# Two token tiles of x transposed one after the other, and a pair's gate product and output norm recorded in later pieces

## The chip, the cores and the metric

The kernel runs on one core of one Trainium2 chip. The metric is the device time of one execution in microseconds (us), lower is better; times below are medians of the runs made, or are read from one profiled execution. Engines are named as the profile names them: PE is TensorE's matrix multiply, PEld its weight load, DVE VectorE, ACT ScalarE, POOL GpSimd and SP SyncE, which here only issues DMAs (SPq is its queue).

## What is computed

Two transformer blocks on one sequence of 256 tokens with 1024 features, all float32. The change lies in the first half of the first block, the mixers. Cut to what matters:

```python
def first_block(x, ...):                                # x [1, 256, 1024]
    xn = rms_norm(x, norm1_gain)
    proj = xn @ w_in                                    # 4*512 retention columns, 1792 rwkv columns
    q, k = rotary(proj[..., 0:512]), rotary(proj[..., 512:1024])
    ret = silu(g_ret) * head_norm(retention(q, k, v), ret_gn_gain)
    rw = rwkv7_time_mix(proj[..., 2048:], ...)
    h = x + concat([ret, rw], -1) @ w_out
    h = h + hier_moe(rms_norm(h, norm2_gain), ...)      # 32 experts, top 2
    return rms_norm(h, final_norm_gain)

def rwkv7_time_mix(feats, ...):                         # 8 heads of 64
    f = feats + (previous_token(feats) - feats) * mu
    r, k, v, w_lo, a_lo, g_lo = split(f)
    decay = exp(-exp(-softplus(-(w0 + tanh(w_lo) @ w_up)) - 0.5))
    a, g = sigmoid(a0 + a_lo @ a_up), sigmoid(g_lo) @ g_up
    y = the recurrence over the tokens (state [64, 64] for each head)
    y = head_norm(y, gn_gain, eps)
    bonus = sum(r * k * r_k, -1) * v
    return (y + bonus) * g
```

The second block (two kinds of attention and a product-key feed-forward) follows on the first one's output.

## The kernel before

The program is one straight run of stages: `phase_a` (the mixers and `w_out`, to about 228 us of the profile), `phase_b` (routing and 32 experts, to about 690 us), then the second block.

Every float32 product that needs full precision is done as three faster matmuls of a high and a low part (`mm3`): ACT copies the high part (line 211 for weights, 349 for x), DVE subtracts to get the low part (218 for weights, 351 for x). Weights come as 128x1024 units over SP's queue (line 204), through a generator `ahead`: each `next(ws)` records the high part of one unit, the low part of the one before it, and the load that takes its buffer.

At the start `setup` issues on SP's queue: the first tile of x (128 tokens), the constants `cst` (the identity for PE's transposes is in it), the gains `vec`, the second tile of x; `phase_a` then the first weight units. `row_rstd` squares each tile of x on ACT (343) for the norm's scale, which later goes in as a row `R` (439). `transposed` transposes x in four banks; each bank holds two 128-feature blocks of all 256 tokens, so its four transposes read both tiles of x; `scaled` then takes a bank out in two 128x256 pieces on ACT (349) and two on DVE (351).

After that the order of the instructions is made by hand-written generators, turned by `interleave`: each generator yields how long (by a running sum of estimated PE time) it wants to stand back, or a condition. Those with the earlier place in the list go first. `features` yields the projection, feature tile after feature tile (24 matmuls of 256 columns each: `xt,u` in the trace; DVE then makes `fe`, `d`, `ft`, lines 525 to 529) and four groups of 512 columns (`u,xt`). `rwkv(p, ...)` for p from 0 to 3 is one pair of heads. It makes its decays from `tl,lora` (`sg`, `cs`, lines 596 to 618), its gate `gg` from `gs,gup` (line 604), takes its k, r and v features (624 to 653), solves a triangular system in five levels (`X`, `Z`, `XT`: 701 to 716), carries a state over four chunks (`G`, `Sb`: 733 to 745), and ends with the head norm of its output: s1 and y on DVE (755 to 757), y² on POOL (759), its sum on DVE (760), the reciprocal root on POOL (336, 338), y·r on DVE (762), then after a yield of 5.5 a transposition back on PE (`cst,y`) and gate, bonus, high and low part (768 to 772). Engines run their instructions in the recorded order, so a DVE instruction that waits holds up all that stand behind it.

`out_weights` loads `w_out` (line 393) when pair 3's front is done, `first_experts` begins the loads of expert weights `wB` (line 890) when pair 2's outputs are recorded. All of these loads are on SP's one queue.

Of the kernel before, what the change touches and what calls it, by code (L numbers as in the profile page):

```python
# [15 lines left out]
AF = mybir.ActivationFunctionType  # L16
# [5 lines left out]
S, D = 256, 1024  # L22
# [60 lines left out]
CST_KEPT = 256  # L83

FM_ORDER = [(12, 13), (4, 0), (8, 5), (9, 1), (2, 10), (11, 6), (7, 3)]
WARM = (8, 0, 4, 0, 0, 5, 14, 2)
# [76 lines left out]
class K:  # L163
# [80 lines left out]
    def mm(self, out, l, r, start=True, stop=True, **k):  # L244
        n = 1
        for x in r.shape[1:]:
            n *= x
        m = 1
        for x in l.shape[1:]:
            m *= x  # L250
        self.pe += (max(n, 64) / 2.4e3 * (1 if l.dtype != F32 else 4) + 0.01) * (1 if m > 64 else 0.5)
        self.nc.tensor.matmul(out, l, r, start=start, stop=stop, **k)  # L252
# [55 lines left out]
    def setup(self):  # L308
        nc, i = self.nc, self.i
# [8 lines left out]
        nc.sync.dma_start(self.h[:, 0], i["x"][:, 0])  # L318
        nc.sync.dma_start(self.cst, i["cst"][:, 0:CST_KEPT])
        nc.sync.dma_start(self.vec, i["vec"])  # L320
        nc.sync.dma_start(self.h[:, 1], i["x"][:, 1])
# [47 lines left out]
    def phase_a(self):  # L369
        nc, tc, i = self.nc, self.tc, self.i  # L370
        with ExitStack() as cx:
# [37 lines left out]
            rt = {"qT": T("late", [128, 2, 4, S], "qT"), "v": T("mid", [128, 2, 512], "vr"), "g": T("late", [128, 2, 512], "gr")}  # L409
            rt["rs"] = [self.row_rstd(self.ap["tiny"], self.h[:, t], rt["v" if t else "g"].rearrange("p t d -> p (t d)"), "rows") for t in range(2)]  # L410
            self.transposed([self.h[:, t] for t in range(2)], "norm1_gain", *xt, ws, WARM[1])
# [151 lines left out]
    def rwkv(self, p, zs, lora, gup):  # L563
# [37 lines left out]
        b = self.bank([128, S])  # L601
        mm(b, gup[:, ps], gs, start=True, stop=True)
        gg = L([128, S], "gg", bufs=NBUF)
        nc.scalar.activation(gg, b, AF.Copy)
# [16 lines left out]
        yield lambda: 4 + p in self.got and p in self.got  # L621
        kp, rp = self.got.pop(4 + p), self.got.pop(p)
# [136 lines left out]
        nc.gpsimd.tensor_tensor(y2, y, y, OP.mult)  # L759
        nc.vector.tensor_reduce(s2, y2, AX.X, OP.add)  # L760
        r = self.rstd(self.ap["end"], s2, 64, 4, RWKV_EPS)
        nc.vector.tensor_tensor(y, y, r[:, :, None].to_broadcast([128, 4, 64]), OP.mult)
        yield 5.5
# [7 lines left out]
        nc.scalar.activation(hi, o, AF.Copy)  # L771
        nc.vector.tensor_tensor(lo, o, hi.bitcast(F32), OP.subtract)
# [1097 lines left out]
```

## Time and profile before

| what | before |
|---|---|
| median of 3 runs | 1635.88 us (1634.16 to 1636.99) |
| the profiled execution | 1633.89 us, of which its span is 1632.1 us |
| PE busy over the span | 1581.5 us (97%), 11118 matmul records |
| DVE busy | 967.6 us (59%) |
| ACT busy | 654.9 us (40%) |
| POOL busy | 218.8 us (13%) |
| read from HBM | 386.62 MB, 238 GB/s over the span |

The span is what the trace covers; 1.8 us of the profiled execution lie around it. A share over the span mixes stages with different limits, so the rows further down are taken by stretch. A row of the timeline gives the start, the time until its last instruction ended, the line and what was written and read, with the number of instructions merged; in square brackets stands how long the engine sat idle before it and what released it.

### The profile page before, as it was taken

Reading aid. Unit: us, or ns where it says so; the run is one execution under the profiler, and the core shown is the slowest. Engines: PE = TensorE matmul, PEld = TensorE weight load, DVE = VectorE, ACT = ScalarE, POOL = GpSimd, SP = SyncE. Lnnn points to the kernel's source line nnn. Section 1 sums busy time; section 2 is a strip of 40 time slices with the busy share of each in tenths; the row PEclk is TensorE's granted clock in tenths of the full one; section 3 lists DMA queues with packets and bytes.
Section 4 is the critical chain, followed back from the end, with each engine's and each line's share of the span. In section 5 each row is a group of like instructions: output and inputs, shape, how many; then the busy total and the mean of one; then the engine's idle time right before and its main releaser. Section 6 shows DMA issues by size and latency. Waiting matters only on the chain.

```text
span 1632.1 us, 28041 instructions
## 1 busy us (share of the span) xinstructions
PE 1581.5 (97%) x11118; PEld 1217.2 (75%) x11118; DVE 967.6 (59%) x1845; ACT 654.9 (40%) x1171; POOL 218.8 (13%) x249
## 2 busy tenths in 40 slices
PE   8999999999999999899999999999999999999998
PEld 7888873443444334378799999999999888888887
DVE  6676561121212112289889997788999755555554
ACT  5333341211111111266655556555544444444443
POOL 3213020000000000174210000123444000000000
PEclk9999999999999999999999999999999999999999
DMA  6324699999999999853355556555555566666664
GB/s 204 105 66 142 228 353 391 405 414 420 419 419 419 420 419 420 345 181 117 98 197 167 188 178 194 162 164 168 162 164 166 169 193 193 193 193 193 194 193 156
DMA packets 84297, 390.61 MB, mean 239 GB/s; under 512 B 9632, under 2 KB 9776, under 8 KB 63424
## 3 DMA queue, kind: packets, MB, share of 16 engines
q1 hardware_dynamic: 83088, 384.45, 65.6%
q0 software_dynamic: 928, 3.25, 0.5%
q8 instruction: 90, 1.47, 0.4%
q10 hardware_dynamic: 144, 1.05, 0.2%
q14 instruction: 47, 0.39, 0.1%
HBM read 386.62 MB, written 2.10 MB: 238 GB/s over the span
## 4 chain that ended last, share of the span: by engine, by line
PE 53%; DVE 2%; POOL 2%; issue 1%; ACT 0%; ACTq 0%; DVEq 0%; POOLq 0%
PE b L252 53%; POOL rs_r L338 1%; DVE u L218 1%; PE b L264 1%; DVE g L1727 0%; POOL rs_m L336 0%; POOL y L1418 0%; POOL rs_r L1407 0%; DVE oh L1835 0%; ACT s L1451 0%; DVE h L469 0%; DVE u L1684 0%; DVE ss L1405 0%; DVE qz L1430 0%; DVE mx L1447 0%
## 5 line engine op out<-in xcount | busy, mean ns | idle before, releaser
L211 ACT ACTIVATE u<-u 128x1024 fp32r<-128x1024 f32 x334 | 354.1, 1061 | 388.2 <-PE b L252 366.2
L218 DVE TENSOR_TENSOR u<-u,u 128x1024 fp32r<-128x1024 f32 x334 | 412.5, 1236 | 150.1 <-PE b L252 114.5
L252 PE MATMUL b<-mix,u 128*128 128x256 f32 x3456 | 425.6, 281 | 0.0
L252 PEld LDWEIGHTS b<-mix,u 128*128 128x128 f32 x3456 | 411.1, 188 | 0.0
L252 PE MATMUL b<-u,oh 128*128 128x512 f32 x1536 | 350.3, 390 | 2.0 <-ACT oh L1667 2.0
L252 PEld LDWEIGHTS b<-u,oh 128*128 128x128 f32 x1536 | 289.3, 188 | 62.8 <-ACT oh L1667 2.2
L252 PE MATMUL b<-mr,u 128*64 128x512 f32 x944 | 232.3, 595 | 16.2 <-DMA mr<-in_wB 16.0
L252 PEld LDWEIGHTS b<-mr,u 128*64 128x64 f32 x944 | 74.5, 137 | 158.0 <-issue 120.7
L1130 DVE TENSOR_TENSOR hh<-hh,b 128x512 f32<-128x512 f32 x16 | 11.0, 688 | 230.2 <-PE b L252 230.2
L1711 POOL TENSOR_TENSOR g<-g,gelu 128x4 f32<-128x4 f32 (+43 forms) x87 | 94.2, 1083 | 355.2 <-ACT gelu L1710 348.2
L252 PE MATMUL b<-u,xt 128*128 128x512 f32 x480 | 123.4, 407 | 0.8 <-DVE u L218 0.8
L252 PE MATMUL b<-mr,hT 128*64 128x512 f32 x480 | 115.5, 596 | 3.6 <-DVEq L1194 1.8
L252 PEld LDWEIGHTS b<-u,xt 128*128 128x128 f32 x480 | 89.1, 191 | 21.5 <-DVE u L218 1.1
L1175 DVE SCALAR_TENSOR_TENSOR u<-b,sw,u 128x512 fp32r<-128x512 f32 x32 | 23.9, 750 | 127.8 <-ACT u L1174 127.8
L252 PEld LDWEIGHTS b<-mr,hT 128*64 128x64 f32 x480 | 35.6, 137 | 70.9 <-issue 63.3
L1155 ACT ACTIVATE hT<-b 128x512 f32<-128x512 f32 x16 | 9.6, 598 | 160.1 <-PE b L264 160.1
L1668 DVE TENSOR_TENSOR oh<-g,oh 128x512 fp32r<-128x512 f32 x64 | 44.3, 693 | 41.1 <-ACT oh L1667 41.0
L1174 ACT ACTIVATE u<-b,sw 128x512 fp32r<-128x512 f32 x32 | 21.9, 687 | 105.1 <-PE b L252 105.1
L1303 POOL MEMSET qz<- 128x2048 f32 x2 | 3.5, 1800 | 448.8 <-DVEq L1194 448.8
L1727 DVE TENSOR_TENSOR g<-g,b 128x252 f32<-128x252 f32 (+47 forms) x111 | 61.5, 592 | 0.0
L1835 DVE TENSOR_TENSOR oh<-oh,gw 128x512 f16<-128x512 f16 x128 | 54.6, 465 | 0.0
L1129 ACT ACTIVATE hh<-b 128x512 f32<-128x512 f32 x16 | 9.6, 597 | 99.3 <-PE b L252 99.3
(381 smaller groups left out, 1713.7 us busy)
## 6 DMA issues: line engine op xcount, KB each, us to landing
mr<-in_wB SPq DMA_DIRECT2D x160, 1024.0 KB, 15.2
u<-in_down SPq DMA_DIRECT2D x128, 512.0 KB, 3.7
u<-in_up SPq DMA_DIRECT2D x128, 512.0 KB, 4.3
mr<-in_wB SPq DMA_DIRECT2D x36, 512.0 KB, 15.0
u<-in_wA SPq DMA_DIRECT2D x30, 512.0 KB, 3.7
u<-in_wB SPq DMA_DIRECT2D x28, 512.0 KB, 14.4
u<-in_wC SPq DMA_DIRECT2D x24, 512.0 KB, 4.0
u<-in_wQ SPq DMA_DIRECT2D x16, 512.0 KB, 3.6
```

What stands on the lines that cost most here:

```text
L211: nc.scalar.activation(hi, r, AF.Copy)
L218: nc.vector.tensor_tensor(lo, r, hi.bitcast(F32), OP.subtract)
L252: self.nc.tensor.matmul(out, l, r, start=start, stop=stop, **k)
L264: self.nc.tensor.transpose(out, x, self.ident)
L338: nc.gpsimd.tensor_tensor(r, m, self.mhalf[:, :width], OP.pow)
L1130: nc.vector.tensor_tensor(self.hh, self.hh, bs[1], OP.mult)
L1174: nc.scalar.activation(yh[:, o], b, AF.Copy, scale=sw)
L1175: nc.vector.scalar_tensor_tensor(yl[:, o], b, sw, yh[:, o].bitcast(F32), op0=OP.mult, op1=OP.subtract)
L1668: nc.vector.tensor_tensor(lo, src, hi.bitcast(F32), OP.subtract)
L1711: nc.gpsimd.tensor_tensor(dst[:, 0:n], dst[:, 0:n], g[:, 0:n], OP.mult)
L1727: nc.vector.tensor_tensor(d, d, s, OP.mult)
L1835: self.nc.vector.tensor_tensor(w[:, :, part].rearrange("p t (k x) -> p t k x", x=2), o[:, :, 0].rearrange("p t (k x) -> p t k x", x=2), se ...
```

## The change

Three places. At the start, SP's queue carries the two tiles of x first, and `cst` and `vec` go on ACT's queue. x is transposed tile by tile: a bank now holds four 128-feature blocks of one tile's 128 tokens, so the first two banks need the first tile alone; each bank is taken out in four 128x128 pieces on each of ACT and DVE (16 on each in place of 8). The squares of x (343) and with them the row scales are recorded behind these. In `rwkv`, the gate product `gs,gup` and its copy move from the pair's decays to the place where its k and r features are there. In the output norm, the one yield of 5.5 becomes 1.0, 2.0 and 1.5 around the sum and y·r, and one of 0.75 stands ahead of the low part.

```diff
-        nc.sync.dma_start(self.h[:, 0], i["x"][:, 0])
-        nc.sync.dma_start(self.cst, i["cst"][:, 0:CST_KEPT])
-        nc.sync.dma_start(self.vec, i["vec"])
-        nc.sync.dma_start(self.h[:, 1], i["x"][:, 1])
+        nc.scalar.dma_start(self.cst, i["cst"][:, 0:CST_KEPT])
+        for t in range(2):
+            nc.sync.dma_start(self.h[:, t], i["x"][:, t])
+        nc.scalar.dma_start(self.vec, i["vec"])
...
+            next(ws)
+            for t in range(2):
+                for k4 in range(2):
+                    b = self.bank([128, 4, 128])
+                    for j in range(4):
+                        k = 4 * k4 + j
+                        self.tr(b[:, j], self.h[:, t, k * 128:k * 128 + 128])
+                    ks, o = range(4 * k4, 4 * k4 + 4), slice(t * 128, t * 128 + 128)
+                    self.scaled(b, [(xt[0][:, k, o], xt[1][:, k, o], self.v("norm1_gain", k)) for k in ks])
+                    if t:
+                        next(ws)
             rt["rs"] = [self.row_rstd(...) for t in range(2)]
-            self.transposed([self.h[:, t] for t in range(2)], "norm1_gain", *xt, ws, WARM[1])
+            next(ws)
+            self.warm(WARM[1])
...
-        b = self.bank([128, S])
-        mm(b, gup[:, ps], gs, start=True, stop=True)
-        gg = L([128, S], "gg", bufs=NBUF)
-        nc.scalar.activation(gg, b, AF.Copy)
...
         yield lambda: 4 + p in self.got and p in self.got
+        b = self.bank([128, S])
+        mm(b, gup[:, ps], gs, start=True, stop=True)
+        gg = L([128, S], "gg", bufs=NBUF)
+        nc.scalar.activation(gg, b, AF.Copy)
...
         nc.gpsimd.tensor_tensor(y2, y, y, OP.mult)
+        yield 1.0
         nc.vector.tensor_reduce(s2, y2, AX.X, OP.add)
         r = self.rstd(self.ap["end"], s2, 64, 4, RWKV_EPS)
+        yield 2.0
         nc.vector.tensor_tensor(y, y, r[:, :, None].to_broadcast([128, 4, 64]), OP.mult)
-        yield 5.5
+        yield 1.5
...
         nc.scalar.activation(hi, o, AF.Copy)
+        yield 0.75
         nc.vector.tensor_tensor(lo, o, hi.bitcast(F32), OP.subtract)
```

Since `interleave` counts estimated PE time, the yields move instructions of other generators too. Three places show how.

On DVE at the end of pair 0's outputs (`y`, `s`, `rs_r` are the norm's, `r` the rotary of a retention tile, `fe` to `ft` a feature tile, `u` a weight's low part, `Z` a level of pair 1's solve), the order before:

```order
L757 TENSOR_TENSOR y_1314<-b_1291,s_1315 128x256
L760 TENSOR_REDUCE s_1316<-y_1320 128x4
L762 TENSOR_TENSOR y_1314<-y_1314,rs_r_1325 128x256
L793 TENSOR_TENSOR r_1241<-b_723,rot_131 128x4x64
L794 TENSOR_TENSOR r_1241<-b_723,rot_131 128x4x64
L525 TENSOR_TENSOR fe_46_223<-b_1254,R_260 128x256
L527 TENSOR_TENSOR d_1358<-fe_46_223 128x256
L529 SCALAR_TENSOR_TENSOR ft_1360<-d_1358,vec_83,fe_46_223 128x256
L218 TENSOR_TENSOR u_1364<-u_995,u_1248 128x1024
L707 TENSOR_TENSOR Z_979<-b_1378,cst_80 128x256
```

and the order now, in the same place on DVE:

```order
L770 TENSOR_TENSOR y_1330<-b_1307,s_1331 128x256
L809 TENSOR_TENSOR r_1257<-b_739,rot_131 128x4x64
L810 TENSOR_TENSOR r_1257<-b_739,rot_131 128x4x64
L774 TENSOR_REDUCE s_1332<-y_1336 128x4
L538 TENSOR_TENSOR fe_46_239<-b_1270,R_276 128x256
L540 TENSOR_TENSOR d_1373<-fe_46_239 128x256
L542 SCALAR_TENSOR_TENSOR ft_1375<-d_1373,vec_83,fe_46_239 128x256
L218 TENSOR_TENSOR u_1379<-u_1011,u_1264 128x1024
L720 TENSOR_TENSOR Z_995<-b_1393,cst_80 128x256
L777 TENSOR_TENSOR y_1330<-y_1330,rs_r_1370 128x256
```

The sum of y² now stands behind the two rotary products, and y·r behind the solve's Z; all else keeps its order.

On ACT at the start (`xt` is the transposed x, `gr` and `vr` are scratch for the squares, `u` a weight's high part), the order before:

```order
L343 ACTIVATE gr_137,ss_138<-h_76 128x1024
L343 ACTIVATE vr_136,ss_144<-h_76 128x1024
L349 ACTIVATE xt_13_133<-b_158,vec_83 128x256 x2
L211 ACTIVATE u_167<-u_150 128x1024
L349 ACTIVATE xt_13_133<-b_169,vec_83 128x256 x2
L211 ACTIVATE u_182<-u_152 128x1024
L349 ACTIVATE xt_13_133<-b_184,vec_83 128x256 x2
L349 ACTIVATE xt_13_133<-b_193,vec_83 128x256 x2
```

and now:

```order
L349 ACTIVATE xt_13_133<-b_146,vec_83 128x128 x4
L349 ACTIVATE xt_13_133<-b_159,vec_83 128x128 x4
L349 ACTIVATE xt_13_133<-b_172,vec_83 128x128 x4
L211 ACTIVATE u_185<-u_138 128x1024
L349 ACTIVATE xt_13_133<-b_187,vec_83 128x128 x4
L211 ACTIVATE u_204<-u_140 128x1024
L343 ACTIVATE gr_137,ss_206<-h_76 128x1024
L343 ACTIVATE vr_136,ss_212<-h_76 128x1024
```

The squares went behind all of x's pieces and two weight units; on DVE all 16 pieces now stand ahead of the first unit's low part.

On SP's queue near the end of the mixers (the last two units of `wA`, and the first of the experts), the order before:

```order
L393 DMA wo_377_2093<-in_wO 128x1024
L890 DMA u_2426<-in_wB 128x1024
L890 DMA u_2427<-in_wB 128x1024
L890 DMA mr_2430<-in_wB 128x1024
L890 DMA mr_2431<-in_wB 128x1024
L890 DMA mr_2434<-in_wB 128x2048
L204 DMA u_2442<-in_wA 128x1024
L204 DMA u_2480<-in_wA 128x1024
L890 DMA mr_2923<-in_wB 128x2048
```

and now:

```order
L393 DMA wo_382_2147<-in_wO 128x1024
L204 DMA u_2291<-in_wA 128x1024
L204 DMA u_2366<-in_wA 128x1024
L906 DMA u_2438<-in_wB 128x1024
L906 DMA u_2439<-in_wB 128x1024
L906 DMA mr_2442<-in_wB 128x1024
L906 DMA mr_2443<-in_wB 128x1024
L906 DMA mr_2446<-in_wB 128x2048
L906 DMA mr_2939<-in_wB 128x2048
```

The two `wA` loads now stand ahead of the first five `wB` loads, not behind them.

## Rows read from the trace of the kernel before

**Rows 1.** By stretch: length, busy PE, PEld, DVE, ACT, POOL, then clock, DMA share, GB/s.
```profile
5.00:10.00 5.00, 2.14 (x9) 1.88 (x10) 0.00 (x0) 2.48 (x6) 3.13 (x8) 1.00 0.96 300
...
40.00:60.00 20.00, 20.00 (x291) 16.66 (x287) 18.99 (x39) 8.86 (x19) 4.90 (x5) 1.00 0.34 107
...
97.00:109.00 12.00, 9.37 (x85) 8.34 (x82) 7.84 (x15) 2.34 (x4) 2.00 (x3) 0.72 0.27 89
109.00:125.00 16.00, 14.44 (x172) 11.94 (x172) 14.31 (x32) 4.95 (x10) 3.33 (x4) 1.00 0.10 34
...
150.00:170.00 20.00, 18.59 (x450) 16.66 (x445) 7.26 (x18) 7.00 (x18) 5.43 (x9) 1.00 0.81 303
```

**Rows 2.** Whom PE waited for, 0 to 240 us: us, times, longest.
```profile
PE b L252 <- DVE Z L707: 3.4, 3, 2.6
```

**Rows 3.** Timeline of the start, all engines: start us, time us, engine, line.
```profile
2.11 0.43 SPq L321 DMA_DIRECT2D h<-in_x  x1
...
8.28 1.06 ACT L343 ACTIVATE vr<-h 128x1024 f32<-128x1024 f32 x1 [2.52 <-DMA h<-in_x]
8.30 3.46 PE L264 MATMUL b<-cst,h 128*128 128x128 f32 x15 [2.81 <-DMA h<-in_x]
...
13.93 2.18 PE L252 MATMUL b<-xt,u 128*128 128x256 f32 x16 [1.74 <-DVE u L218]
...
23.00 0.67 PE L252 MATMUL b<-gs,gup 128*128 128x256 f32 x2 [1.68 <-issue]
...
32.89 0.70 PE L252 MATMUL b<-rk,cst 128*128 128x256 f32 x2 [0.15 <-DVE rk L631]
```

**Rows 4.** DVE groups by form in the mixers: busy us, mean ns of one.
```profile
L351 DVE SCALAR_TENSOR_TENSOR xt<-b,vec,xt 128x256 fp32r<-128x256 f32 x8 | 3.4, 477 | 9.9 <-ACT xt L349 9.9
L745 DVE TENSOR_SCALAR Sb<-b,gam 128x64 f32<-128x64 f32 x12 | 3.4, 280 | 4.9 <-PE b L252 4.9
```

**Rows 5.** Timeline of DVE around pair 0's output norm.
```profile
95.56 0.42 DVE L760 TENSOR_REDUCE s<-y 128x4 f32<-128x256 f32 x1 [0.73 <-POOL y L759]
97.43 0.43 DVE L762 TENSOR_TENSOR y<-y,rs_r 128x256 f32<-128x256 f32 x1 [1.45 <-POOL rs_r L338]
...
101.28 0.41 DVE L707 TENSOR_TENSOR Z<-b,cst 128x256 f32<-128x256 f32 x1
...
109.70 0.30 DVE L599 TENSOR_SCALAR sg<-sg 128x256 f32<-128x256 f32 x1 [1.64 <-ACT sg L596]
```

**Rows 6.** Timeline of PE in the same place.
```profile
97.15 2.06 PE L252 MATMUL b<-xt,u 128*128 128x256 f32 x15
101.84 1.12 PE L252 MATMUL b<-XT,Z 64*64 64x64 f32 x16 [2.63 <-DVE Z L707]
...
121.14 0.33 PE L252 MATMUL b<-Sb,G 64*64 64x64 f32 x4 [1.43 <-DVE Sb L745]
```

**Rows 7.** PE in half-microseconds: first and last slice with a lowered clock.
```profile
101.00:101.50 0.50, 0.00 (x0) 0.91 0.00 0
...
108.00:108.50 0.50, 0.50 (x2) 0.76 0.00 0
```

**Rows 8.** Timeline of SP's queue near the end of the mixers.
```profile
173.10 1.63 SPq L890 DMA_DIRECT2D mr<-in_wB  x3
178.33 2.06 SPq L204 DMA_DIRECT2D u<-in_wA  x2
190.30 3.79 SPq L890 DMA_DIRECT2D mr<-in_wB  x3
```

**Rows 9.** By stretch, columns as in rows 1: the weight stream's pauses, and the experts.
```profile
185.00:190.00 5.00, 5.00 (x65) 3.77 (x65) 1.51 (x2) 2.44 (x3) 0.00 (x0) 1.00 0.01 3
...
240.00:245.00 5.00, 5.00 (x29) 2.40 (x29) 3.70 (x16) 2.64 (x5) 0.00 (x0) 1.00 0.51 179
245.00:250.00 5.00, 5.00 (x26) 1.72 (x24) 0.00 (x0) 0.60 (x1) 0.00 (x0) 1.00 0.60 189
...
500.00:600.00 100.00, 91.73 (x436) 38.69 (x434) 17.50 (x33) 16.67 (x33) 0.00 (x0) 1.00 1.01 420
```

## Prediction, made before the changed kernel ran

> **What bounds the kernel now.** I read the busy times by stretch first, then the list of whom PE waited for, then the timelines of the places that list names, then the weight stream. In the mixers PE is the bound: from 40 to 60 us it shows 20.00 of 20 us busy, [rows 1], and its timeline has no wait between 33 and 97 us. DVE is close behind, 18.99 of 20 us in that stretch and 14.31 of 16 us from 109 to 125 us [rows 1], so a gain on PE lasts only as far as DVE can follow. After the start PE's waits are few: 3.4 us in three for the solve's Z, of which one is 2.63 us, and 1.43 us for a state Sb [rows 2, 6]. The large one, at 99.2 to 101.84 us, has a second cost: the granted clock leaves 1.0 (2.4 GHz) in the slice at 101.0 and is back after the slice at 108.0 [rows 7], some 6.8 us at 0.5 (1.2 GHz), and the whole stretch from 97 to 109 us averages 0.72 [rows 1]. In the start PE waits 2.81 us for the second tile of x, 1.74 us for the first weight's low part and 1.68 us ahead of the gate product [rows 3].
>
> Whether time saved in the mixers reaches the end depends on the weight stream. From 250 us the DMA engines are full (1.01 at 500 to 600 us, where PE shows only 91.73 of 100), so the experts end when their weights have landed. But at 240 to 250 us the stream pauses, with a share of 0.51 and 0.60 [rows 9]: all buffers are full, and it starts again only as PE frees them. So the experts begin with PE, and the saved time passes through, one for one, as long as the loads ahead of that pause land early enough too.
>
> **Step 1, the start.** Before, the first bank needs both tiles, so PE stands until the second one lands, at 8.30 us, 6.2 us after its issue at 2.11 [rows 3]. Now eight transposes (8 x 3.46/15 = 1.85 us [rows 3]) and eight pieces on ACT and DVE lie ahead of that. The issue moves from fourth place to second, about 0.9 us up, at 0.43 us and a little more an issue [rows 3]. The DMA engines, however, are 0.96 busy from 5 to 10 us [rows 1], and the same bytes of x, cst and vec are under way, so I take 0.5 us of it: landing at 7.8 (estimate; bounds 6.5 and 8.3).
> The Trainium skill, "DMA: Bandwidth & Descriptors", section "Issuing engines are not separate DMA queues", speaks against this edit: DMAs from several engines run on the same 16 DMA engines, and another issuer saves only issue time. By that rule landing would stay near 8.3 and the sum below would be 0.5 less, which is inside my range; the 0.96 share agrees with it.
> The smaller pieces cost: eight of 256 columns are busy 3.4 us on DVE, 0.42 us each [rows 4], and I count ACT's like them. A 128-column piece isn't in the trace. Half the price is one end (0.21), the same price the other (0.42); a 64-column DVE instruction takes 0.280 us where the 256-column one takes 0.477 [rows 4], which makes me take 0.27: 16 x 0.27 = 4.3 us, some 1 us more on each engine. Behind the second tile then stand four transposes (0.9), four pieces (1.1), a weight's high part (1.06, a 128x1024 ACT row like that of [rows 3]), four pieces (1.1), four on DVE (1.1) and the first low part, which now stands behind all pieces (1.2): 7.8 + 6.5 = 14.3 us, where it was 13.93 [rows 3]. So PE's first feature tile begins 0.4 later. What is won is behind it: the gate product leaves the place where PE waited 1.68 us, and its own 0.67 us [rows 3] comes back two feature tiles later, when its input is long there. 1.68 - 0.4 = 1.3 us. At 32.89 us PE waits for DVE's rk already [rows 3], and DVE has 1 us more to do but starts its pieces some 3 us earlier; I take 0.3 off. **Term 1: 1.0 us gained** (-0.5 with the late landing and the dear pieces, 2.0 with the early and cheap ones).
> The squares and row scales come later, behind two weight units; they are needed only after two thirds of the first feature tile, about 16.4 us. Two squares (2 x 1.06, from about 13) and two POOL steps end at about 16.1, so they cost nothing, with 0.3 us to spare. The issue of two DMAs on ACT is hidden: ACT has nothing else to do until the first bank is transposed.
>
> **Step 2, pair 0's norm.** DVE stood 0.73 us for y² and 1.45 us for the root [rows 5], with Z behind it in the queue. Now the two rotary products stand in the first of these gaps, a feature tile and a weight's low part in the second, and y·r (0.43) goes behind Z. Nothing else was added ahead of Z, so Z is done 0.73 + 1.45 + 0.43 = 2.6 us earlier, at 101.69 - 2.6 = 99.1 us, while PE comes for it at 97.15 + 2.06 = 99.2 us [rows 5, 6]. On POOL the root now stands behind the two rotary steps (0.7 us each, estimate from POOL's like steps); it is due behind Z only. I leave PE a wait of 0.2, so 2.4 us go. With the wait goes the clock's fall: 6.8 us at half clock are 3.4 us of PE's work. Behind that PE runs against the copies on ACT: DVE's sg waited 1.64 us for ACT [rows 5], and the copies of mix, rhs and sg keep their order there. I take 0.7 off. **Term 2: 2.4 + 3.4 - 0.7 = 5.1 us** (2.2 if only DVE's own waits go and the clock still falls, 6.0 if all goes).
>
> **Step 3, pair 1's norm and pair 2's front.** From 109 to 125 us DVE has 14.31 of 16 us [rows 1], and no instruction leaves it; the 1.43 us wait for Sb [rows 6] stays, since two feature tiles and pair 2's reciprocal still stand ahead of that Sb. Only later, around 137 us, is the second wait for Z (0.6, of the 3.4 in [rows 2]) covered by the same reordering. **Term 3: 0.6** (-1.0 to 2.0).
>
> **Step 4, the two last solves.** From 150 to 170 us PE is busy 18.59 of 20 us [rows 1], 1.4 us of small waits, where only solves stand on it; the new order puts feature matmuls between their last levels. **Term 4: 0.4** (-0.6 to 1.3). At the end pair 3's transposition now stands directly ahead of the w_out product; its high and low part are due 5.7 us later, behind two of the eight slices of w_out (24 matmuls each), against DVE work of about 5. That is covered by 0.7 us; were it not, it would cost up to 1.
>
> **Step 5, SP's queue.** Five wB loads now stand behind the last two wA loads. The stream is idle from 185 to 190 us (0.01 [rows 9]), so a late one lands there. No cost.
>
> **The sum.** 1.0 + 5.1 + 0.6 + 0.4 = 7.1 us. The profiled execution took 1633.89 us (span 1632.1 and 1.8 around it); less 7.1 it is 1626.8. It lies 2.0 below the median of the runs, so against 1635.88 the forecast is **1628.8 us**.
>
> **The rivals.**
> A. The clock falls in the start instead. After the transposes PE has two matmuls (they need only high parts) and then stands for the first low part, by step 1 from about 11.7 to 14.3 us, with about 1 us of standing before them. Against it: 2.81 us at 5.5 to 8.3 did not lower the clock (1.00 from 5 to 10 us [rows 1]). For it: 2.63 us at 99.2 did [rows 7]. Two feature tiles at half clock cost 3.4 us, of which 0.4 would hide behind DVE: 7.1 - 3.0 = 4.1 us, 1631.8.
> B. The stream caps the gain. If the loads before the pause don't move up with PE, only the pause can be used up: 5 x 0.49 + 5 x 0.40 = 4.4 us, 1631.5. Against it: these loads wait for PE and DVE themselves, and everything I save lies before them.
> C. DVE is the true bound, and what PE gains before 109 us is taken back from 109 to 125, where DVE was full: no gain, 1635.9. Against it: DVE's work there began late as well, waiting 1.64 us for ACT [rows 5], so it moves up.
> D. Slower. The two wA loads wait for a weight buffer, and now hold five wB loads behind them, the seven together 4.2 MB (six of 0.52 and one of 1.05), 10.0 us at the 420 GB/s of [rows 9]. Before they went out at 178.33, five us after the wB loads at 173.10, and the next ones went at 190.30 [rows 8]. If the buffers come free only when the stream is full again, after 190, then 10.0 us less the 4.4 of the pause come out as delay: 5.6 slower, 1641.5. It decides at about 185 us. Against it: feature matmuls move forward in the new order, so buffers come free earlier.
>
> **How the numbers follow.** Forecast 0.50, A 0.27, B 0.10, C 0.08, D 0.05. The forecast's own range is 1624.8 (7.1 and about half of the upper spread of the terms) to 1632.5. A reaches 1634.5 with its lower bounds; C and D stay out, so the range is 1624.8 to 1634.5. A measurement tells a difference of about 0.2% (3.3 us). Faster by more: 0.46 of the forecast, 0.18 of A, 0.07 of B, together 0.71. Within it: 0.04, 0.09, 0.03 and 0.07 of C, 0.23. Slower: D and a hundredth of C, 0.06.
>
> **What would show it.** Step 1: the second tile of x released at 7.5 to 8 us, the first full feature tile at about 14.3, no wait ahead of the gate product, pair 0's rk product about 1 us earlier than 32.89, and a clock of 1.00 from 10 to 20 us (A: about 0.5 to 0.7). Step 2: no wait over 0.5 us for Z near 98 us, a clock of 1.00 from 95 to 110, and pair 2's sg at about 103.5 in place of 109.70. Steps 3 and 4: the Sb wait stays, the waits from 150 to 170 shrink. Stream: the pause still there, about 7 us earlier. The prediction is wrong if a new wait of PE over 2 us appears, or if the lead at 125 us isn't there at 228.

## The result: slower, and the profile after

The changed kernel takes 1647.68 us (median of 7 runs, 1645.76 to 1653.49), the kernel before 1637.21 (7 runs): a ratio of 1.0065, 95% interval 1.0050 to 1.0081. The forecast was 1628.8, the range ended at 1634.5. The profiled execution took 1646.35 us, 1644.6 of it span, 12.5 more than the one before; by the medians the loss is 10.5.

By stretch, the changed kernel (columns as in [rows 1]):

```profile
10.00:20.00 10.00, 6.53 (x37) 6.24 (x38) 6.52 (x17) 7.22 (x13) 3.88 (x5) 0.66 0.72 244
20.00:30.00 10.00, 5.52 (x29) 4.96 (x29) 4.32 (x10) 3.03 (x6) 4.98 (x13) 0.73 0.45 145
97.00:109.00 12.00, 11.87 (x197) 10.86 (x193) 10.71 (x22) 3.05 (x5) 3.55 (x5) 1.00 0.29 91
140.00:150.00 10.00, 7.40 (x91) 5.94 (x88) 5.60 (x13) 4.70 (x12) 1.57 (x2) 0.87 0.06 16
150.00:170.00 20.00, 16.79 (x348) 15.24 (x347) 10.13 (x22) 4.87 (x13) 5.86 (x9) 0.89 0.23 84
```

and two stretches of the kernel before that [rows 1] leaves out:

```profile
20.00:30.00 10.00, 8.28 (x63) 7.58 (x62) 8.49 (x19) 7.08 (x14) 2.79 (x6) 1.00 0.63 202
140.00:150.00 10.00, 10.00 (x183) 8.67 (x184) 9.15 (x18) 2.38 (x5) 2.87 (x3) 1.00 0.32 107
```

Against these and [rows 1], the stretch from 97 to 109 us is mended, as forecast: 11.87 us busy in place of 9.37, clock 1.00 in place of 0.72. But 20 to 30 us is half empty, 140 to 150 has lost 2.60 us of PE, and the clock is down in four of these five. Whom PE waited for up to 240 us, where [rows 2] has the Z of before (us, times, longest):

```profile
PE b L252 <- ACT u L211: 6.0, 2, 3.4
PE b L252 <- ACT tl L545: 4.5, 1, 4.5
PE b L252 <- DVE Z L720: 2.6, 1, 2.6
```

Of the 6.0 us of the first line 2.60 are no wait for a weight: they are the wait at 147.12 below, of a matmul that reads Z, done at 146.98, and XT, done at 141.52. The wait for `tl` is new, and its cause stands on POOL's timeline in the start:

```profile
13.99 0.27 POOL L336 TENSOR_SCALAR rs_m<-ss 128x1 f32<-128x1 f32 x1 [5.31 <-ACT gr L343]
16.14 1.42 POOL L338 TENSOR_TENSOR rows<-rs_m,mhalf 128x1 f32<-128x1 f32 x1
17.52 0.61 POOL L426 DMA_DIRECT2D wr<-in_wr  x1
23.75 0.66 POOL L428 TENSOR_TENSOR wr<-wr,vec 128x288 f32<-128x288 f32 x1 [5.62 <-DMA wr<-in_wr]
25.45 0.55 POOL L560 MEMSET tl<- 128x512 f32 x1
26.03 0.42 ACT L545 ACTIVATE tl<-ft 64x256 f32<-64x256 f32 x1 [7.18 <-POOL tl L560]
26.50 2.08 PE L252 MATMUL b<-tl,lora 128*128 128x256 f32 x4 [4.48 <-ACT tl L545]
```

The same queue before:

```profile
10.30 0.61 POOL L413 DMA_DIRECT2D wr<-in_wr  x1
15.92 1.21 POOL L415 TENSOR_TENSOR wr<-wr,vec 128x288 f32<-128x288 f32 x1 [5.01 <-DMA wr<-in_wr]
18.16 0.55 POOL L547 MEMSET tl<- 128x512 f32 x1
```

The row scales wait for the squares, which now come late. Behind them in POOL's queue stands the load of the router's weights `wr`, then a product that waits for this load to land, then the zeroing of `tl`, into which ACT writes pair 0's decay input. Before, `wr` was issued 7.2 us earlier, and `tl` was zeroed 7.3 us earlier. So ACT stood 7.18 us for `tl`, and PE 4.48, and from 24.6 to 31.4 us the clock was down.

Behind pair 0 the gain is there, and then it is lost twice over. Beginning of the head norm of each pair's outputs on DVE (its first sum), and of the `w_out` product on PE, in us:

| profiled execution | pair 0 | pair 1 | pair 2 | pair 3 | w_out |
|---|---|---|---|---|---|
| before | 93.74 | 124.89 | 173.06 | 190.38 | 205.09 |
| changed | 99.95 | 127.81 | 185.48 | 210.35 | 216.90 |

6.2 us late at pair 0, 2.9 at pair 1 in spite of a slightly longer wait for Sb (2.02 us in place of the 1.43 of [rows 6]), 12.4 at pair 2. PE in between:

```profile
147.12 0.33 PE L252 MATMUL b<-Z,XT 64*64 64x64 f32 x4 [2.60 <-ACT u L211]
155.48 0.33 PE L252 MATMUL b<-Z,XT 64*64 64x64 f32 x4 [2.55 <-DVE Z L720]
```

where the kernel before has one such wait of 0.60,

```profile
137.30 0.33 PE L252 MATMUL b<-Z,XT 64*64 64x64 f32 x4 [0.60 <-DVE Z L707]
```

and DVE ahead of the first of them:

```profile
142.42 0.30 DVE L612 TENSOR_SCALAR sg<-sg 128x256 f32<-128x256 f32 x1 [2.91 <-ACT sg L609]
...
144.54 0.35 DVE L639 TENSOR_SCALAR kr<-ft,vec 128x256 f32<-128x256 f32 x1
144.81 0.35 DVE L641 TENSOR_SCALAR k<-av,vec 128x256 f32<-128x256 f32 x1
145.19 0.93 DVE L642 SCALAR_TENSOR_TENSOR k<-k,ft 128x256 f32<-128x256 f32 x1
146.16 0.48 DVE L644 SCALAR_TENSOR_TENSOR rk<-k,vec,ft 128x256 f32<-128x256 f32 x1
146.56 0.42 DVE L720 TENSOR_TENSOR Z<-b,cst 128x256 f32<-128x256 f32 x1
```

Z is a level of pair 2's solve. Ahead of it stand pair 3's decays, the first of which waits 2.91 us for ACT, and all of its k features. Before, Z stood ahead of these features:

```profile
136.74 0.42 DVE L707 TENSOR_TENSOR Z<-b,cst 128x256 f32<-128x256 f32 x1
137.07 0.34 DVE L626 TENSOR_SCALAR kr<-ft,vec 128x256 f32<-128x256 f32 x1
```

Ahead of the next one, at 154.92, stand pair 3's reciprocal (151.32, 1.75 us) and five products behind it. Each wait was followed by a stretch at 1.2 GHz, 147 to 151 and 157 to 162 us by one-us slices. Of the 9.5 us lost between pairs 1 and 2, 2.60 + 2.55 less the 0.60 of before are waiting for Z, 0.53 is waiting for an X behind it, and the clock's two stretches of 3.4 us cost half of that each, 3.4 together: 8.5. The other 1.0 is not placed.

In these two executions the delay then passes through: the experts begin 11.9 us later (241.09 and 253.00), the span ends 12.5 later.

### The profile page after: what moved, and what is told of

It reads as the page before. It is cut to its first block, busy times and chain, and to the rows that moved or that the text cites. A ratio compares the mean times of both kernels' runs of the same rounds, so it can differ in the third digit from the quotient of the medians.

```text
span 1644.6 us, 28056 instructions
## 1 busy us (share of the span) xinstructions
PE 1586.8 (96%) x11118; PEld 1220.7 (74%) x11118; DVE 970.1 (59%) x1853; ACT 656.0 (40%) x1179; POOL 221.2 (13%) x249
## 4 chain that ended last, share of the span: by engine, by line
PE 53%; DVE 2%; POOL 2%; issue 1%; ACT 1%; ACTq 0%; DVEq 0%; POOLq 0%
PE b L252 52%; POOL rs_r L338 1%; DVE u L218 1%; PE b L264 1%; DVE g L1743 0%; POOL rs_m L336 0%; POOL y L1434 0%; POOL rs_r L1423 0%; DVE oh L1851 0%; ACT s L1467 0%; DVE h L482 0%; DVE u L1700 0%; DVE ss L1421 0%; DVE qz L1446 0%; DVE mx L1463 0%
## 5 line engine op out<-in xcount | busy, mean ns | idle before, releaser
L252 PE MATMUL b<-xt,u 128*128 128x256 f32 x336 | 49.1, 302 | 5.9 <-ACT u L211 3.4
```

## The experiments

Each ratio is against the kernel before, run beside it on the same chip, with its 95% interval. Single executions of one kernel lie up to 10 us apart, so what is under 3 us rests on the intervals alone.

### The start alone

```diff
 # before, with the start as changed; norm and gate product as before
```

> Before plus the start alone (order of the first DMAs, tile-by-tile transposition, squares behind it); norm and gate product stay as before. Theory (the late row scales hold POOL's queue, so the product on the router weights waits for its DMA and the zeroing of tl stands behind it): the two POOL row scales end near 17.5 us, the router product near 24, PE waits 4 to 5 us for tl, the outputs of pair 0 come 5.5 to 6.5 us later than before, and about 5 to 6 us of that reach the end: 1642.5 to 1643.5 against 1637.2. Rival (the start is a gain of 1 us as predicted and the whole loss comes from the norm): 1636.

1642.36 us, ratio 1.0044 (1.0032 to 1.0056): 7.1 over the kernel before. PE waits 3.59 us for `tl`, pair 0's outputs come at 100.58 (6.8 late), `w_out` at 210.51 (5.4 late). The start loses, a little more than expected.

### The start undone

```diff
 # changed, with the start of before
```

> The changed kernel with the start of before; norm and gate product as changed. PE's order behind the start is that of the changed kernel. Theory (start costs about 6, pair 0's norm gives 5, the later order of pairs 1 to 3 costs about 10): 5 to 6 us under the changed kernel, so 1641 to 1642.5, still 4 to 5 us over before; PE's waits for Z near 141 and 149 us (147 and 155 less 6) stay above 2 us each with a clock under 1.00 behind them. Rival (only the start loses; the later waits are its echo, since the late start lets pair 3's front and pair 2's solve meet): 1632, and the granted clock 1.00 from 140 to 165 us.

1642.91 us, 1.0049 (1.0030 to 1.0068). Pair 0 at 94.33, pair 1 at 122.20 (2.7 ahead of before: pair 0's norm pays), pair 2 at 178.24 (5.2 behind). The waits for Z stay (2.61 at 141.51, 2.42 at 149.74). So the second loss needs no late start. But the start undone was to give 5 to 6 us against the changed kernel; by the two ratios it gave 2.6, and the intervals overlap. What the start costs beside the other parts is less than its 7.1 alone.

### The router's weights behind the zeroing

```diff
-            nc.gpsimd.dma_start(self.wr, i["wr"])
-            (product on wr, load of br)
             zs = self.rwkv_setup()
+            nc.gpsimd.dma_start(self.wr, i["wr"])
+            (product on wr, load of br)
```

> The changed kernel with one move on POOL's queue: the load of the router weights, the product on them and the load of their bias stand behind the zeroing of sg and tl and the mask. Theory: tl is zeroed near 19 us, PE's wait of 4.48 us for tl and the fall of the clock at 24 us go, 4 to 5.5 us are won against the changed kernel: 1642 to 1643.5; the fall of the clock at 11 us stays, since that has another cause (the two first matmuls and the wait for the first low part). Rival (the loss of the start is the clock's fall at 11 us and the small pieces): within 1 us of the changed kernel, 1647.

1644.35 us, 1.0051 (1.0031 to 1.0072); the interval overlaps the changed kernel's, so the time alone doesn't settle it. The trace does: the wait for `tl` and the fall of the clock behind it are gone, pair 0 is at 95.53 (4.4 earlier), `w_out` at 211.00 (5.9 earlier). By the two ratios it gives 2.3 us; its profiled execution was the fastest of the five. DVE's first feature `fe` stands 2.73 us for PE and begins at 20.03, where the profile before has 18.23:

```profile
14.42 3.78 PE L252 MATMUL b<-xt,u 128*128 128x256 f32 x16 [2.83 <-DVE u L218]
20.03 0.42 DVE L538 TENSOR_TENSOR fe<-b,R 128x256 f32<-128x256 f32 x1 [2.73 <-PE b L252]
```

PE's 16 matmuls take 3.78 us there in place of the 2.18 of [rows 3]. That, and the 1.8 us left at pair 0, can't be put down to the changed start: runs with the start of before show as much (see step 1 below).

### Pair 0's norm alone

```diff
-        yield 5.5
+        yield 1.5 if p == 0 else 5.5      # with the 1.0, 2.0 and 0.75 for p == 0 too
```

> Before plus the split norm for pair 0 alone (pairs 1 to 3 keep the one yield of 5.5); PE's order is that of before to the last instruction. Theory (the gain at pair 0's norm is real and lasts; the loss comes from what the new yields do to pairs 1 to 3): no wait over 0.5 us for Z near 99 us, clock 1.00 from 97 to 109 us, 4 to 5.5 us gained, 1632 to 1633. Rival (DVE bounds the stretch from 109 to 125 us and takes it back): the wait for Sb grows from 1.43 to over 3 us and the time is within 1.5 us of before, 1636 to 1638.

1630.44 us, 0.9965 (0.9950 to 0.9980), and 1633.10, 0.9974 (0.9962 to 0.9987) on another chip, of which was expected:

> The split norm for pair 0 alone once more, on the chip of the other three for a direct comparison. Theory (all later versions keep its gain and add little): 1630 to 1632.5, within 2 us of the version with the repaired start and the gate product. Rival (the repaired start is worth 2 us or more): over 2 us above that version.

4.8 and 4.0 us faster than before; the second time is 0.6 above its expected range, and 1.7 above the version with the repaired start and the gate product at the end of this section. The stretch that the change was after:

```profile
97.00:109.00 12.00, 11.87 (x165) 10.55 (x162) 10.43 (x25) 5.07 (x10) 3.54 (x5) 1.00 0.39 122
```

No wait for Z there, clock 1.00, and the Sb wait stays at its 1.4. Step 2 of the prediction stands.

### The gate product alone

```diff
         yield lambda: 4 + p in self.got and p in self.got
+        (gate product and copy, from the decays)
```

> Before plus the gate product's move alone (start and norm as before). Theory (the move is nearly neutral; in the start it takes 1.68 us of waiting off PE, but DVE bounds 20 to 60 us, so the outputs of pair 0 move by less than 1 us): 1634.5 to 1636.5 against 1635.2. Rival (the move itself sends rk, sq and the gate's copy into worse places and costs in pair 1 to 3): 1638 or more, with a new wait of PE over 1 us for rk or Z.

1643.61 us, 1.0054 (1.0037 to 1.0070): the theory fell. I had taken this move for free. In its trace pair 2's Z comes 2.61 us late at 138.72, with pair 3's four k features ahead of it on DVE, which stood behind it before. And at pair 3 PE waits 4.35 us for Sb, behind this on DVE and POOL:

```profile
178.73 0.42 DVE L762 TENSOR_TENSOR y<-y,rs_r 128x256 f32<-128x256 f32 x1 [1.45 <-POOL rs_r L338]
185.22 0.56 DVE L817 TENSOR_TENSOR st<-b,st 128x384 f32<-128x384 f32 x1 [6.06 <-PE b L252]
...
189.58 0.28 DVE L745 TENSOR_SCALAR Sb<-b,gam 128x64 f32<-128x64 f32 x1
```

```profile
177.66 1.04 POOL L338 TENSOR_TENSOR rs_r<-rs_m,mhalf 128x4 f32<-128x4 f32 x1
178.67 1.16 POOL L812 DMA_DIRECT2D st<-in_retd  x2
```

In the kernel before:

```profile
159.09 2.28 POOL L812 DMA_DIRECT2D st<-in_retd  x4
```

The row at 185.22 names PE, but it multiplies the retention's scores by the decay masks `st`, and the last two of their four loads left POOL's queue only at 178.67, behind pair 2's root, where all four went out from 159.09 before; such a load takes 6.0 us here. From 185 to 200 us PE has 10.65 of 15 us at a clock of 0.77.

### Pair 1's norm alone

```diff
+        (1.0, 2.0, 1.5 and 0.75 for p == 1 only)
```

> Before plus the split norm for pair 1 alone. Theory (this one split is what loses after 125 us: it flags pair 1 as done later, so pair 3's front is recorded one solve level later and stands ahead of two Zs of pair 2 on DVE): outputs of pairs 0 and 1 at the times of before, 93.7 and 124.9 us; two waits of PE for Z or its neighbours of about 2.5 us each between 138 and 155 us with the granted clock under 1.00 behind them; outputs of pair 2 some 7 to 8 us late; 1642 to 1643.5 against 1635.2. Rival (the later order alone is harmless, the loss needs the start or the gate product too): 1634.5 to 1637.

1650.43 us, 1.0093 (1.0077 to 1.0110), twice the expected loss. Pair 3's front is recorded only when pair 1 is flagged as done (`("all", p - 2) in self.done`). With the split, that flag comes later, pair 3's front is recorded a level later, and PE waits for pair 2's Z, and for pair 3's further down, where the masks stand in the way again:

```profile
151.38 0.34 PE L252 MATMUL b<-Z,XT 64*64 64x64 f32 x4 [2.95 <-DVE Z L707]
179.07 0.33 PE L252 MATMUL b<-Z,XT 64*64 64x64 f32 x4 [1.92 <-DVE Z L707]
187.05 0.68 PE L252 MATMUL b<-XT,Z 64*64 64x64 f32 x16 [2.42 <-DVE Z L707]
```

```profile
184.88 0.56 DVE L823 TENSOR_TENSOR st<-b,st 128x384 f32<-128x384 f32 x1 [5.96 <-DMA st<-in_retd]
```

The parts don't add up: 7.7 for the gate product and 14.5 here, less 4.8 for pair 0, would be 17.4, and the two parts together (start undone) lose 7.7. Each makes another order out of the rest.

### All norms but pair 1's

```diff
+        (1.0, 2.0, 1.5 and 0.75 for p != 1)
```

> Before plus the split norm for pairs 0, 2 and 3, pair 1 with the one yield of 5.5. Theory: pair 0's gain of 5 us stays, pairs 2 and 3 stand where only long matmuls run and change nothing: 1629.5 to 1631.5. Rival (pair 3's split takes cover from the low part at the end, up to 1 us and more): 1632 to 1634, with a wait of PE over 1 us at the w_out product.

1633.07 us, 0.9985 (0.9974 to 0.9996): a gain, without pair 1's split. It came 1.6 us above the expected range and into the rival's, but without the rival's wait at the `w_out` product; whether pairs 2 and 3 cost a little is not settled.

### Pair 1 split, order kept

```diff
+        (0.5, 1.0 and 1.0 for p == 1, none ahead of the low part)
```

> Before plus the split norm for pair 0 (1.0, 2.0, 1.5, 0.75) and for pair 1 with shorter yields (0.5, 1.0, 1.0 and none ahead of the low part), so that PE's order is that of before to the last instruction; against the run with pair 0 alone, only pair 1's sum and y*r stand later on DVE. Theory (what pair 1's split lost was the later place of pair 3's front, not the split): 1629.5 to 1631.5, 4 to 6 us under before, and no wait for Z over 1 us between 125 and 190 us. Rival (the split itself sets pair 1's outputs back): 1634 or more.

1633.26 us, 0.9975 (0.9962 to 0.9987), above the 1629.5 to 1631.5 expected but under the rival's 1634, and with no wait for Z over 0.6 us. A split at the same places that lost 14.5 us, with shorter yields and none ahead of the low part, loses nothing that can be measured: PE's order stays.

### The gate product with the masks early

```diff
+        yield lambda: ("tm", 0) in self.done
+        (the four loads of the decay masks)
         yield lambda: ("tm", 1) in self.done
```

> The gate product's move alone, as in the run before, with one more edit: the four loads of the retention's decay masks are issued on POOL's queue when the first retention group is turned, about 60 us earlier, and PE's and DVE's orders stay as they were. Theory (the 8 us that the move lost came from DVE standing 6.06 us for these masks, which POOL issued behind pair 2's root at 178.67; Sb stood behind that, PE waited 4.35 us and the clock fell from 188 to 195): the wait for Sb at 189.9 is under 1 us, no clock under 1.00 from 185 to 200 us, 1636 to 1638. Rival (the loss is in the order on PE and DVE itself, the waits for rk and Z of 1.2 and 2.6 us): 1642 to 1644.

1639.44 us, 1.0018 (1.0001 to 1.0034): 4.2 us of the 7.7 back (5.9 by the two ratios), less than expected. The Sb wait of 4.35 us is gone. Pair 2's Z still waits 2.61 us at 140.12: the masks were part of it, some half or more, and the order on DVE the rest.

### Three repairs on the change

```diff
 # changed, with the two moves on POOL above, pair 1's short yields,
 # and the one yield of 5.5 for pairs 2 and 3
```

> The start and the gate product as changed, the split norm for pair 0 as changed and for pair 1 with the short yields (pairs 2 and 3 with the one yield of 5.5), and the three repairs together: the router weights behind the zeroing on POOL, the decay masks loaded early, pair 3's front at its old place. Theory (these three are the whole loss): outputs of pair 0 about 1.8 us late as in the run with the router weights moved, the 5 us of pair 0's norm on top, 1631 to 1634. Rival (something else in the change loses too): 1637 or more.

1638.04 us, 1.0017 (1.0000 to 1.0035): 7.9 us under the changed kernel by the two ratios, but the rival's number: something else lost too. PE still waits 2.61 and 1.04 us for Z, at 136 and 143; the gate product's order, not yet known as a cause, was left as changed.

### The gate product, order kept

```diff
         nc.scalar.activation(gg, b, AF.Copy)
+        yield 0.0
         kp, rp = self.got.pop(4 + p), self.got.pop(p)
```

> The gate product's move alone, with a yield of 0.0 recorded right behind its copy: the other generators get a turn there, and the orders on DVE and POOL are those of before to the last instruction; on ACT and PE only the gate product and its copy stand elsewhere (12 of PE's matmuls change places). Theory (the move itself is free, its loss of 8 us came from the turn that fell away: pair 3's kr to rk ahead of pair 2's Z, the decay masks' loads behind pair 2's root): 1634 to 1636.5 against 1635.9. Rival (the gate product or its copy costs in its new place): 1638 or more.

1636.33 us, 0.9993 (0.9981 to 1.0005). One empty yield, which gives the other generators their turn, takes the whole loss away: kr to rk stand behind Z again, the masks ahead of the root. The product itself is free in its new place, and no gain: PE's wait of 1.68 us ahead of it is gone, but PE waits 1.24 us for rk at 33.59, where it waited 0.15 [rows 3].

### All three parts, order kept

```diff
 # as the three repairs, but the gate product with its yield of 0.0
 # in place of the early masks
```

> The three parts of the change with the order of before kept: the start as changed with the router weights behind the zeroing on POOL, the gate product's move with the yield of 0.0, the split norm for pair 0 as changed and for pair 1 with the short yields. Theory (each part's own work is nearly free or a gain, the loss was queue order): the start costs 0 to 2 us, pair 0's norm gives 5, so 1631 to 1634, 13 to 16 under the changed kernel. Rival (the start's small pieces and its waits cost 4 us or more by themselves): 1635 or more.

1633.44 us, 0.9975 (0.9963 to 0.9987), 3.6 us faster than before and 0.3 above pair 0's norm alone on the same chip (1633.10). Its start still has PE waiting 2.78 and 2.54 us with the clock down from 10 to 18; since the time is that of pair 0's norm alone, the new start, with POOL's queue in order, the gate product and pair 1's split together neither cost nor give what can be measured.

### The start repaired, and the best of all

```diff
+            rt["rs"] = [(square and scale of the first tile)]
             next(ws)
             (tile by tile; next(ws) behind banks 2 and 3; 12 warming matmuls behind the transposes)
+            rt["rs"].append((square and scale of the second tile))
 # and the router's weights behind the zeroing
```

> The split norm for pair 0 alone, with the changed start repaired: the first tile's square stands ahead of the pieces on ACT, the second's right behind them, the first weight's high part behind the first tile's pieces and its low part on DVE ahead of the last four pieces, 12 warming matmuls fill PE's wait, and POOL takes the router weights behind the zeroing. Theory (what the new start lost was the order behind the pieces, not the pieces): the first feature tile starts at about 12.5 us in place of 13.9, the first fe on DVE at 16 to 17 in place of 18.23, outputs of pair 0 at 92 to 93 in place of 93.74, 1628.5 to 1630. Rival (16 small pieces and a slowed POOL eat the lead): outputs of pair 0 at 94 or later and the time of the pair 0 norm alone, 1630.4, or up to 2 us more.

With pair 0's norm: 1631.17 us, 0.9977 (0.9967 to 0.9987), the rival's time and not the 1628.5 to 1630 expected. The first feature tile starts at 12.92 in place of 13.93 [rows 3], but the first `fe` only at 17.90, not at 16 to 17:

```profile
8.71 0.56 POOL L338 TENSOR_TENSOR rows<-rs_m,mhalf 128x1 f32<-128x1 f32 x1
13.95 1.51 POOL L338 TENSOR_TENSOR rows<-rs_m,mhalf 128x1 f32<-128x1 f32 x1
12.92 2.87 PE L252 MATMUL b<-xt,u 128*128 128x256 f32 x16 [1.52 <-DVE u L218]
15.59 1.05 PE L252 MATMUL b<-cst,rows 128*128 128x128 f32 x4
```

The same root takes 0.56 us in one place and 1.51 in the other, but it does not hold PE: it ends at 15.46, and PE comes for the rows at 15.59 without standing. The lead goes to the clock, which is down from 14.1 to 17.5 us: the first 16 matmuls take 2.87 us where [rows 3] has 2.18 (3.55 and 3.65 in the next two runs). Pair 0 is at 93.85, no earlier than in the profile before, though 0.7 ahead of the middle of the other runs with the old start (94.56); the time doesn't show it. The same with pair 1's short yields:

> The repaired start with the split norms of pairs 0 and 1 in the order of before. Theory: as the repaired start with pair 0's norm, 1631.2, or up to 1 us less, since pair 1's y*r leaves DVE's way at 127 us: 1629.5 to 1631.5. Rival (pair 1's split costs by itself): 1633 or more.

1630.47 us, 0.9966 (0.9950 to 0.9982), as expected. And with the gate product in its new place, order kept:

> The repaired start, the split norms of pairs 0 and 1 and the gate product's move with the order kept. Theory: PE's wait of 1.57 us for gs in the start goes, but DVE bounds the stretch behind it, so 0 to 1 us under the repaired start with both norms (1630.5): 1629 to 1631. Rival (the copy of the gate on ACT stands in the way of the squares sq and PE waits for rk): 1632 or more.

1631.37 us, 0.9969 (0.9957 to 0.9982), 0.4 above the expected range: 5.7 us under before on its chip and, by the ratios, 15.7 under the changed kernel. Its interval overlaps that of pair 0's norm alone, so nearly all of the gain is that norm's; the rest is not shown.

## Why the prediction was wrong, step by step

Its own sign of being wrong came: a new wait of PE over 2 us, the 4.48 for `tl`. Steps 1, 3 and 4 failed.

**Step 1** failed, in the sentence that the squares and row scales "cost nothing, with 0.3 us to spare". Of its 1.0 us gained, 1.68 were the gate product's, and the start itself was to cost 0.4; alone it lost 7.1. The first full tile began at 14.27 (14.3 forecast), but by two errors that cancel: the second tile released PE at 6.49, before the 7.8 assumed (and before the 8.3 of the other case in the prediction), and what stands behind it took 7.8 us, not 6.5, because `vec`, now on ACT's queue, landed at 6.7 and held ACT's first piece. (The small pieces cost what was assumed: 16 of them keep DVE busy for 4.3 us.) The row scales ended at 17.56, not 16.1, because the two roots took 1.43 and 1.42 us where the trace before has 0.57 and 0.55. Even so PE came for them at 17.82 without standing. What they held was POOL's queue: I followed the moved step to the row R and not down that queue, past the `wr` load and the product that waits for it, to `tl`.

Rival A, the clock's fall in the start, shows in the changed kernel (0.66 from 10 to 20 us), but it is not the loss: the version with all parts in order has it too and is faster than before. Nor is it a mark of the change. In the nine other runs that have the start of before, the first 16 feature matmuls take 2.75 to 3.78 us, as in pair 0's norm alone:

```profile
14.70 3.78 PE L252 MATMUL b<-xt,u 128*128 128x256 f32 x16 [1.74 <-DVE u L218]
```

Only the profile that the prediction was read from has 2.18. In those nine runs the first `fe` begins at 18.71 to 20.72 and pair 0's outputs at 93.89 to 96.69, where that profile has 18.23 and 93.74: one execution was too few to read a baseline from. A's price was mis-summed as well: a feature tile is 3.0 us of PE's work at full clock (72 matmuls, three tiles, take 8.98 us from 23.32 on in the trace before), so two at half clock cost 6.0, not 3.4.

**The gate product** stood inside step 1 as 1.68 us gained, less 0.3 for rk. Most of the 1.68 came back as the wait for rk. And its place in pair 0 was read, but what the moved code does to the turns of pairs 2 and 3 was not: 7.7 us alone, nothing with the turn given back.

**Step 2** was right in its mechanism: 5.1 forecast, 4.8 and 4.0 measured alone. That the size came so close is partly luck. Its 3.4 for the clock was read from a fall of 6.8 us; in the five other runs that keep this wait of 2.63 us (the start, the gate product and pair 1's norm alone, the masks early, the gate product with its order kept) the recorded fall lasts 3.4 us, which is worth 1.7. In the changed kernel pair 0's lag of 6.2 us has shrunk to 1.0 by pair 2's decays (108.90 us).

**Step 3** failed in sign. With "no instruction leaves it" the wait of 1.43 us for Sb was to stay, and it is 2.02; the Z near 137 us, which was to be covered, waits 2.60. The runs place both: in all six that have the gate product in its new place without the yield of 0.0, Sb waits 2.0 us and this Z 2.6; in all others Sb waits 1.4 and this Z at most 0.6. So it is the gate product, and not the norms, that step 3 overlooked.

**Step 4** (0.4 gained) failed most: "the new order puts feature matmuls between their last levels" read PE's order and not what stands ahead of Z on DVE at the same places. Alone, pair 1's split is a loss of 14.5 us, and the second of the two waits for Z, at 155.48, comes with it: it is 1.49 to 2.95 us in the four runs that have this split as changed, and at most 1.04 in all others.

**Step 5** held, as far as a run that is some 12 us late there can show it. The two `wA` loads went out at 179.10, the five `wB` loads behind them from 184.72 on, in the stretch that was a gap in [rows 9]:

```profile
179.10 5.58 SPq L204 DMA_DIRECT2D u<-in_wA  x2
184.72 0.91 SPq L906 DMA_DIRECT2D u<-in_wB  x2
```

```profile
185.00:190.00 5.00, 5.00 (x76) 3.87 (x71) 2.82 (x6) 1.72 (x3) 1.84 (x3) 1.00 0.90 256
240.00:245.00 5.00, 5.00 (x46) 4.87 (x45) 4.61 (x12) 3.46 (x6) 1.24 (x3) 1.00 1.01 418
```

The gap is not filled but has moved: from 200 to 210 us the DMA share is 0.02 and 0.00. So has the pause at 240 us, now from 255 to 265 us, behind the experts' beginning at 253, and shallower (0.90 and 0.83).

**The rivals.** The slower case, D, had the wrong place (SP's queue) and 0.05. The two causes that decided were in no rival: a wait for a load inside POOL's queue, and a Z behind another pair's front.

## What to carry to other kernels

A step that is moved later takes with it all that stands behind it on its queue: follow the queue down to the next instruction that some busy engine waits for, through every load that is issued and waited for on the way. Where generators share a running sum of time, one yield more or less, even an empty one, sets the order of everything after it: diff the order of every engine to the end, and read off what now stands ahead of each short product on which a chain depends. Read a baseline from more than one execution: the start of the one profile used here was the exception. When one part of a change gains, try it with the order of the rest held fixed; here that kept the 4 to 5 us and avoided losses of 7.1, 7.7 and 14.5.

## What the runs showed of the hardware

A small POOL instruction takes 0.55 us or 1.43 (the 128x1 root in the start, before and changed). The long ones began at 14.35, 16.14 and (repaired start) 13.95 us, while DVE made a weight's low part, and each ended 0.41 to 0.44 us after that low part did; the short ones ran beside DVE's pieces of x or while it stood. The Trainium skill, "SBUF — State Buffer", section "SBUF: two separate sides", says that DVE and GpSimd share a pair of ports as an exclusive lock: of a DVE instruction with two SBUF inputs and a GpSimd one that reads SBUF, the one that starts first holds it for its whole length and the other waits. That agrees: the low part has two SBUF inputs and takes 1.22 us, a piece of x reads one from PSUM. No run here varies that input alone.

The recorded clock can miss a fall. In the run with the start alone, the stretch from 10 to 20 us shows 1.00, yet its first 16 feature matmuls take 3.78 us, where they took 2.18 before [rows 3] and 3.72 in the changed kernel, whose record shows the fall. Four more runs show 1.00 from 10 to 20 us and 3.49 to 3.78 us (pair 0's norm alone, the gate product alone and with its order kept, all norms but pair 1's):

```profile
14.61 3.78 PE L252 MATMUL b<-xt,u 128*128 128x256 f32 x16 [2.53 <-DVE u L218]
10.00:20.00 10.00, 6.19 (x27) 5.90 (x28) 6.15 (x16) 7.55 (x15) 3.88 (x5) 1.00 0.62 220
```

The Trainium skill, "TensorE: Matmul & The Clock Gate", section "Seeing it yourself", warns that recorded clock events have been observed to be unreliable on trn2 and should not be fully trusted one by one. The matmuls' durations above bear that out.

The fall itself is not certain either. Behind the same wait of 2.63 us for Z near 102 us the recorded clock was down for 6.8 us in the kernel before and for 3.4 us in the runs of the gate product alone and of pair 1's norm alone; behind the 2.0 us wait for Sb it fell in the changed kernel (123 to 127 us) and by the record not in the gate product's run. That may be part of why single executions of one kernel differ; no run here shows how large a part.
